# Moving the sums of the down-projection weights in a Strassen-Winograd feed-forward on one Trainium2 core

## The chip, the core and the metric

One core of a Trainium2 chip runs the whole program. The metric is device microseconds of one execution, start to end. The engines work side by side and each takes its instructions in the order written for it: TensorE (PE: matmuls; PEld: its weight loads), VectorE (DVE), ScalarE (ACT), GpSimd (POOL) and SyncE (SP), which issues all the transfers of this kernel. Engines wait for one another by semaphores. SBUF is the on-chip memory of 128 partitions, PSUM holds the matmul results in eight banks, DRAM is the memory outside.

## The reference

Two encoder layers of width 1024 run over 1024 prompt rows and 8 x 16 sample rows (1152 rows, nine tiles of 128). Each layer is attention, then a channel mixer; every sub-layer is modulated by a condition (adaLN) and closed by a scaled residual and a layer norm. The change lies in the channel mixer:

```python
u = h @ w_up                                  # 1024 -> 2 x 2816
y = conv_b + sum(conv_w[tap] * ue[:, tap:tap + T] for tap in range(3))
a, g = jnp.split(y, 2, axis=-1)
out = (jax.nn.gelu(g) * a) @ w_down           # 2816 -> 1024
x = layer_norm(DEEPNORM_ALPHA * x + (1 + g_f) * out, ln_g, ln_b)
```

`ue` is `u` with two earlier rows ahead of it. All is float32.

## The kernel before

**Precision.** Each matmul operand is split into a high part (a cast, by ScalarE, line 177) and a low remainder (a subtraction, mostly by VectorE, line 188), and each product is three matmuls: low x high, high x low, high x high. `wh`, `wl` are the two parts of weights, `xa`, `H` and `x2r` hold those of activations.

**The up stage** (`ffn`). The 2816 columns of each half of w_up are 22 blocks of 128; block j of the first half and block j of the gate half form pair j. Pairs 0 and 1 are computed plainly. Then `tsums` forms sums of the transposed activations, and pairs 2 to 21 run as a Strassen-Winograd scheme with seven half-sized products (`products`). A pair starts with two loads of 512 KB (lines 1369 and 1370, into a ring of four buffers, so two pairs), GpSimd forms four sums of weights (lines 1177 to 1180), and for each product the weight is split into one of six slots, TensorE does 2 x 12 matmuls (line 1229), and ScalarE or VectorE takes the two results out of PSUM, adding what is there (lines 1188, 1190, 1197). When a half of the pair is complete, `conv_row` applies the convolution (ScalarE line 1316, VectorE line 1277 for two taps, GpSimd line 1286 for sample rows), and `gated` does the GELU (ScalarE, line 1323) and the gating (GpSimd, line 1324) and stores the row block.

**Preparation for the down stage, done in the up stage.** The down-projection is Winograd's scheme too. `act_sums` forms, for two finished blocks, four sums of activations on GpSimd (lines 1336 to 1339) and stores them to `actS`. `weight_sums(m)` does it for blocks 2m and 2m+1 of w_down, with lo and hi halves of 512 columns: b11, b12 are the halves of block 2m, b21, b22 those of block 2m+1. It loads both blocks into the two buffers `w0` (tile w0f, line 1347), forms four sums in place on GpSimd (lines 1348 to 1351), and stores both buffers to the DRAM tensor `wT` (line 1353). It is called inside pair `wsum[m]` behind its third product; `wsum` is 2, 3, 4, 6, 8, ... 20. There is one pair of `w0` buffers, so set m+1 loads when set m is stored.

**The down stage** (`down`). Seven products run one after another, numbered 1, 2, 5, 6, 3, 7, 4, each over the eleven m, with four banks of prompt rows and, in products 1, 2, 5 and 6, a fifth for the sample rows. `fetch(q, m)` loads an activation operand and a weight half, splits them, and returns them. A weight half goes either into a buffer of the rings `early` and `late`, or, for stored sums, straight into the slot that its low part will take; there are six slots in products 1 to 6. Product 5 takes `wT[m, 0]`'s lo half for prompt rows and the hi half of block 2m for sample rows. Behind the products follow the residual and norm of each tile of 128 rows (`head`, `tail`); `homes` says into which buffer each tile's residual row block is loaded (line 1081). In layer 1 `tail` (lines 1530 to 1534 and 1004 to 1019) writes the output.

**Order.** The program is written in the order above, and a planner then orders each engine's instructions with a simulated timeline: an instruction whose inputs and buffers are ready may be placed ahead of others written before it. `issue_after(ins)` adds an edge that keeps those instructions of a block that run on the engine of `ins` behind `ins`. In layer 0 the adaLN weights of later stages are loaded and multiplied between the products (lines 226 and 234), and 16 copies of a bias table run (line 1657).

Of the kernel before, what the change touches and what calls it, by code (L numbers as in the profile page):

```python
# [102 lines left out]
class Trunk:  # L103
# [1140 lines left out]
    def ffn(self, l, xsrc, xdst, affs):  # L1244
        nc, I, O, H, F = self.nc, self.I, self.O, self.H, self.F
# [67 lines left out]
        def conv_row(u, j, gg, y):  # L1313
            cc = j + 22 * gg
            tap = tapper(cc)
            nc.scalar.activation(y, u[:, 2:1154], AF.Identity, bias=cw[:, cc, 3:4], scale=cw[:, cc, 2:3])  # L1316
            tap(y[:, 0:1024], u[:, 1:1025], 1)
            tap(y[:, 0:1024], u[:, 0:1024], 0)
            samples(y[:, 1024:1152], u[:, 1026:1154], cc, tap)
            rows(j, gg, u[:, 1024:1168])  # L1320

        def gated(j, ya, yg):
            nc.scalar.activation(yg, yg, AF.Gelu_apprx_tanh)
            nc.gpsimd.tensor_mul(yg, yg, ya)  # L1324
            if j % 2:
                nc.sync.dma_start(self.actD[j], yg)
                self.pend.append(j // 2)
            else:
                for r in (slice(0, 512), slice(1024, 1152)):
                    nc.sync.dma_start(self.actD[j][:, r], yg[:, r])  # L1330

        def act_sums():
            for m in self.pend:
                a11, a21 = ygate[0][:, 0:512], ygate[0][:, 512:1024]
                a12, a22 = ygate[1][:, 0:512], ygate[1][:, 512:1024]
                nc.gpsimd.tensor_add(a22, a21, a22)
                nc.gpsimd.tensor_sub(a21, a11, a21)
                nc.gpsimd.tensor_sub(a11, a22, a11)
                nc.gpsimd.tensor_sub(a12, a12, a11)
                for i in range(2):  # L1340
                    nc.sync.dma_start(self.actS[m, i], ygate[i][:, 0:1024])
            self.pend = []

        def weight_sums(m):
            b11, b12, b21, b22 = (t[:, o : o + 512] for t in self.w0 for o in (0, 512))
            for i in range(2):
                nc.sync.dma_start(self.w0[i], I["wdn"][l, 2 * m + i])
            nc.gpsimd.tensor_sub(b11, b12, b11)
            nc.gpsimd.tensor_sub(b12, b22, b12)
            nc.gpsimd.tensor_sub(b22, b22, b11)  # L1350
            nc.gpsimd.tensor_sub(b21, b22, b21)
            for i in range(2):
                nc.sync.dma_start(self.wT[l][m, i], self.w0[i])

        def plain(j):
            y = [yact, ygate[j % 2]]
# [10 lines left out]
        def spair(j):  # L1367
            sa, sg = self.ws.next(), self.ws.next()
            nc.sync.dma_start(sa, I["wup"][l, j])
            nc.sync.dma_start(sg, I["wup"][l, j + 22])  # L1370
            ua, ug = us.next(), us.next()
            y = []

            def after(i, q):
                if i % 2 == 0:
                    self.step(1)
                if i == 1:
                    act_sums()
                if i == 2 and j in wsum:
                    weight_sums(wsum.index(j))  # L1380
                if q == 4:
                    y.append(ygate[j % 2])
                    conv_row(ug, j, 1, y[0])

            self.products(sa, sg, ua, ug, (S1, S2, S3), p1s, sub, TT, after, "first" if j == NPL else None)
            ya = yact
            conv_row(ua, j, 0, ya)
            gated(j, ya, y[0])

        self.pend = []  # L1390
        wsum = [2, 3] + list(range(4, NFF - 1, 2))
# [9 lines left out]
        for j in range(NPL, NFF):  # L1401
            spair(j)
            if l == 0 and j == 2:
                self.tables_b(self.ws.next())
            if l == 0 and 3 <= j < 19:
                with self.tc.issue_after(self.pairmm):
                    self.skew_b(j - 3)
# [4 lines left out]
    def down(self, l, xsrc, xdst, affs, act_sums):  # L1412
        nc, I, F, H = self.nc, self.I, self.F, self.H
# [13 lines left out]
        narrow = self.ws  # L1427
        fa, fb = F[:, 4096:5120], F[:, 8320:9344]
        homes = {8: fa, 0: fb, 1: self.w0[1], 2: fa, 3: fb, 4: X2[:, 0:1024], 5: X2[:, 2048:3072], 6: fa, 7: fb}
        xs = {}  # L1430

        def rows(*ts):
# [3 lines left out]
        raws = [w[:, i * 512 : i * 512 + 512] for w in [self.w0[1]] + narrow.items for i in range(2)]  # L1436
        early = Ring(raws + [F[:, o : o + 512] for o in (0, 512, 1024)])
        late = Ring(raws)
        subs = self.subslots(ws[1:4])
        X1 = self.X1  # L1440
        acts = Ring([(X1[:, o : o + 640], X1[:, o + 640 : o + 1280]) for o in range(0, 8960, 1280)])
# [2 lines left out]
        wdn, wT, actD, actS = I["wdn"][l], self.wT[l], self.actD, self.actS  # L1444
        lo_half, hi_half = slice(0, 512), slice(512, 1024)

        def weight(src, ring=None):
            hi, lo = subs.next()
            raw = ring.next() if ring else lo.bitcast(F32)
            nc.sync.dma_start(raw, src)  # L1450
            self.split(raw, hi, lo, "a", "v")
            return hi, lo

        def act(src, sample=None):
            n = 512 if sample is None else 640
            hi, lo = (t[:, 0:n] for t in acts.next())
            raw = lo.bitcast(F32)
            nc.sync.dma_start(raw[:, 0:512], src)
            if sample is not None:
                nc.sync.dma_start(raw[:, 512:640], sample)  # L1460
            self.split(raw, hi, lo, "a", "v")
            return hi, lo
# [12 lines left out]
        def prompt(j, n):  # L1475
            return actD[j][:, n]

        def sample(j):
            return actD[j][:, 1024:1152]

        def fetch(q, m):
            e, o = 2 * m, 2 * m + 1
            w2 = None
            if q == 1:
                a, w = act(prompt(e, lo_half), sample(e)), weight(wdn[e][:, lo_half], early)
            elif q == 2:
                a, w = act(prompt(o, lo_half), sample(o)), weight(wdn[o][:, lo_half], early)
            elif q == 5:
                a, w = act(actS[m, 1][:, hi_half], sample(e)), weight(wT[m, 0][:, lo_half])
                w2 = weight(wdn[e][:, hi_half], late)  # L1490
            elif q == 6:
                a, w = act(actS[m, 0][:, lo_half], sample(o)), weight(wT[m, 1][:, hi_half])
                w2 = weight(wdn[o][:, hi_half], late)
            elif q == 3:
                a, w = act(actS[m, 1][:, lo_half]), weight(wdn[o][:, hi_half], late)
            elif q == 7:
                a, w = act(actS[m, 0][:, hi_half]), weight(wT[m, 0][:, hi_half])
            else:
                a, w = act(prompt(o, hi_half)), weight(wT[m, 1][:, lo_half])
            return a, w, w2 or w  # L1500

        def product(q, banks, bs=None, new=True, keep=0, hook=None):
            for m in range(NK - keep):
                a, w, w2 = fetch(q, m)
                for i in range(4):
                    mm(self.bank(banks[i]), a, i, w, new and m == 0, m == NK - 1)
                if bs is not None:
                    mm(self.bank(bs), a, 4, w2, q in (1, 5) and m == 0, q in (2, 6) and m == NK - 1)
                if hook:
                    hook(m)  # L1510
# [85 lines left out]
        subs = Ring(subs.items + more)  # L1596
# [15 lines left out]
        subs = Ring(subs.items[0 : NK - len(more)] + more if l == 0 else subs.items)  # L1612
        product(4, E, keep=keep, hook=tails(2))
        kept = [(m, fetch(4, m)) for m in range(NK - keep, NK)]
        for i in range(4):
            for m, (a, w, _) in kept:
# [303 lines left out]
```

## Time and profile before

| what | us |
|---|---|
| median of 3 runs | 2839.86 (2837.35 to 2843.75) |
| the profiled execution | 2844.65 |
| its span, first to last instruction | 2842.6 |
| TensorE busy | 2676.1 (94%) |
| VectorE busy | 2027.0 (71%) |
| ScalarE busy | 1348.0 (47%) |
| GpSimd busy | 1106.9 (39%) |
| DMA queue, share of 16 engines | 56.8% |

The up stage's pair loops run from 537.6 to about 1062 us (layer 0) and from 2075.3 to about 2566 us (layer 1), the down stages behind them to about 1345 and to the end. Rows of the profile name an engine, a line of the kernel, the operation, and what it writes and reads; the number behind an x is a count. In rows of stretches stand first the stretch and its length, then the busy time of each engine, then the clock granted to TensorE, the DMA engines' share and their rate. In square brackets stands how long the engine was idle before an instruction and what ended that. A row "A <- B: t, n, m" of the waits says that A waited for B t us in n waits, the longest m.

### The profile page before, as it was taken

How to read it: one execution, taken by the hardware profiler on the slowest of the kernel's cores; microseconds unless marked ns; L12 is line 12 of the kernel's file. 1: busy time of each engine (PE TensorE's matmuls, PEld its weight loads, DVE VectorE, ACT ScalarE, POOL GpSimd, SP SyncE). 2: the span in 40 equal slices, each digit the busy share in tenths (PEclk: the TensorE clock that was granted, in tenths of full speed). 3: DMA queues.
4: the chain of work that ended last, by engine and by line, in shares of the span. 5: the costliest groups of instructions: out<-in, count | busy, mean ns of one | idle time of the engine just before them, and what ended most of it. 6: DMA issues, size and time to landing. Idle time of an engine off the chain costs nothing. (4 is left out here: it accounts for less than half of the span.)

```text
span 2842.6 us, 47206 instructions
## 1 busy us (share of the span) xinstructions
PE 2676.1 (94%) x17134; PEld 2356.5 (83%) x17134; DVE 2027.0 (71%) x3850; ACT 1348.0 (47%) x2752; POOL 1106.9 (39%) x808
## 2 busy tenths in 40 slices
PE   7999889889999999999899999999988999999997
PEld 5897768878999997777798888767988999997775
DVE  4376767777776684588663677668888888885578
ACT  3475724433333344455636666652443344444454
POOL 2132523678554641013421111232489855551001
PEclk9999999999999999999999999999999999999998
DMA  8656434698554447675767457854565422237664
GB/s 291 213 159 197 141 129 156 209 329 283 183 175 156 163 133 236 225 248 196 267 201 257 122 156 198 225 162 146 178 206 196 177 81 96 85 116 239 216 218 156
DMA packets 252714, 534.35 MB, mean 188 GB/s; under 512 B 40032, under 2 KB 100400, under 8 KB 252480
## 3 DMA queue, kind: packets, MB, share of 16 engines
q1 hardware_dynamic: 252480, 531.32, 56.8%
q8 instruction: 135, 2.21, 0.3%
q14 instruction: 99, 0.81, 0.1%
HBM read 391.12 MB, written 149.54 MB: 190 GB/s over the span
## 5 line engine op out<-in xcount | busy, mean ns | idle before, releaser
L1229 PE MATMUL PS<-H,wh 128*128 128x256 f32 (+1 forms) x2624 | 409.7, 299 | 0.0
L1466 PE MATMUL PS<-wh,xa 128*128 128x512 f32 x1144 | 366.9, 399 | 11.9 <-DVE F L1584 5.3
L1229 PEld LDWEIGHTS PS<-H,wh 128*128 128x128 f32 x2624 | 374.4, 193 | 0.0
L1277 DVE SCALAR_TENSOR_TENSOR F<-F 128x1024 f32<-128x1024 f32 x320 | 312.9, 1025 | 28.1 <-ACT F L1316 27.8
L177 ACT CAST wh<-F 128x512 fp32r<-128x512 f32 (+2 forms) x234 | 137.1, 594 | 316.5 <-PE PS L1229 203.7
L1190 DVE TENSOR_TENSOR F<-PS,F 128x320 f32<-128x320 f32 (+1 forms) x446 | 196.6, 451 | 123.5 <-PE PS L1229 121.6
L188 DVE TENSOR_TENSOR wl<-F,wh 128x512 fp32r<-128x512 f32 (+2 forms) x234 | 238.6, 1029 | 56.0 <-ACT wh L177 54.3
L1466 PEld LDWEIGHTS PS<-wh,xa 128*128 128x128 f32 x1144 | 215.4, 189 | 69.5 <-ACT H L177 6.1
L1229 PE MATMUL PS<-H,wl 128*128 128x256 f32 (+1 forms) x1312 | 235.4, 301 | 24.4 <-ACT F L1197 15.3
L1466 PE MATMUL PS<-wl,xa 128*128 128x512 f32 x572 | 227.0, 397 | 0.2
L1229 PEld LDWEIGHTS PS<-H,wl 128*128 128x128 f32 x1312 | 196.6, 193 | 34.3 <-ACT F L1197 16.3
L1229 PE MATMUL PS<-xa,wh 128*128 128x320 f32 (+1 forms) x1328 | 207.5, 299 | 0.0
L188 DVE TENSOR_TENSOR xa<-xa 128x640 fp32r<-128x640 f32 (+1 forms) x154 | 122.5, 801 | 112.8 <-ACT xa L177 112.3
L1229 PEld LDWEIGHTS PS<-xa,wh 128*128 128x128 f32 x1328 | 189.8, 192 | 0.0
L1065 POOL TENSOR_TENSOR F<-F 128x1024 f32<-128x1024 f32 x24 | 62.7, 2611 | 308.2 <-ACT xa L177 148.9
L177 ACT CAST xa<-xa 128x640 fp32r<-128x640 f32 (+1 forms) x154 | 104.0, 682 | 162.8 <-DMA xa<-actD 110.8
L188 DVE TENSOR_TENSOR wl<-ws,wh 128x512 fp32r<-128x512 f32 (+1 forms) x149 | 166.2, 1120 | 10.3 <-ACT wh L177 10.2
L1316 ACT ACTIVATE F<-F 128x1152 f32<-128x1152 f32 x80 | 108.0, 1351 | 114.7 <-DVE F L1190 65.7
L177 ACT CAST wh<-ws 128x512 fp32r<-128x512 f32 (+1 forms) x167 | 113.1, 685 | 102.9 <-PE PS L1229 47.1
L640 POOL TENSOR_TENSOR F<-F,x2r 64x512 f32<-64x512 f32 x62 | 79.4, 1280 | 167.9 <-DVE F L616 145.6
L1324 POOL TENSOR_TENSOR F<-F 128x1152 f32<-128x1152 f32 x44 | 123.7, 2810 | 52.1 <-DVE F L1277 40.8
L1229 PE MATMUL PS<-xa,wl 128*128 128x320 f32 (+1 forms) x664 | 122.9, 307 | 21.2 <-DVE F L1190 20.7
(346 smaller groups left out, 6287.3 us busy)
## 6 DMA issues: line engine op xcount, KB each, us to landing
ws<-in_adaw_dram SPq DMA_DIRECT2D x64, 512.0 KB
ws<-in_wup_dram SPq DMA_DIRECT2D x49, 512.0 KB
F<-in_adaw_dram SPq DMA_DIRECT2D x48, 512.0 KB
w0f<-in_wdn_dram SPq DMA_DIRECT2D x44, 512.0 KB
wT<-w0f SPq DMA_DIRECT2D x44, 512.0 KB
actS<-F SPq DMA_DIRECT2D x44, 512.0 KB
xa<-actS SPq DMA_DIRECT2D x88, 256.0 KB
F<-in_wup_dram SPq DMA_DIRECT2D x39, 512.0 KB
```

The lines of the kernel that those rows point to most:

```text
L177: nc.scalar.copy(out, in_)
L188: self.eng(el).tensor_sub(lo, src, hi.bitcast(F32))
L640: self.eng("v" if last else "p").tensor_mul(on[r, q], on[r, q], rb[r, :])
L1065: self.eng(er[0]).tensor_mul(xr, x, self.lng)
L1190: nc.vector.tensor_add(d, v(ps), a if len(a.shape) == 3 else v(a))
L1229: self.pairmm = nc.tensor.matmul(ps[:, 0:m], w[a][:, k * 128 : k * 128 + 128], x(p, k, n), start=start and c == 0, stop=c == 11, skip_grou ...
L1277: nc.vector.scalar_tensor_tensor(o, u, cw[:, cc, i : i + 1], o, op0=ALU.mult, op1=ALU.add)
L1316: nc.scalar.activation(y, u[:, 2:1154], AF.Identity, bias=cw[:, cc, 3:4], scale=cw[:, cc, 2:3])
L1324: nc.gpsimd.tensor_mul(yg, yg, ya)
L1466: self.downmm = nc.tensor.matmul(ps, a[p][:, i * 128 : i * 128 + 128], w[q], start=first and c == 0, stop=last and c == 2, skip_group_chec ...
```

## The change

In `weight_sums` the instruction that formed the difference b12 - b11 is gone. b12 becomes b22 - b12, b22 becomes that plus b11, which is what b22 - (b12 - b11) was, and b21 becomes b22 - b21: three sums. Of block 2m's buffer only the hi half is stored. The call stands under an `issue_after` on the second load of its own pair, so that the set's loads and stores come behind that load on SP's queue; GpSimd's instructions get no such edge. In the down stage, product 5 loads both halves of block 2m of w_down into a ring of eight buffers, GpSimd forms the difference, and both are split as before. In layer 1 the residual row blocks 6 and 7 get buffers of their own in place of those of blocks 2 and 3.

```diff
             for i in range(2):
                 nc.sync.dma_start(self.w0[i], I["wdn"][l, 2 * m + i])
-            nc.gpsimd.tensor_sub(b11, b12, b11)
             nc.gpsimd.tensor_sub(b12, b22, b12)
-            nc.gpsimd.tensor_sub(b22, b22, b11)
+            nc.gpsimd.tensor_add(b22, b12, b11)
             nc.gpsimd.tensor_sub(b21, b22, b21)
-            for i in range(2):
-                nc.sync.dma_start(self.wT[l][m, i], self.w0[i])
+            nc.sync.dma_start(self.wT[l][m, 0][:, 512:1024], b12)
+            nc.sync.dma_start(self.wT[l][m, 1], self.w0[1])
...
-            nc.sync.dma_start(sg, I["wup"][l, j + 22])
+            pairdma = nc.sync.dma_start(sg, I["wup"][l, j + 22]).ins
...
                 if i == 2 and j in wsum:
-                    weight_sums(wsum.index(j))
+                    with self.tc.issue_after(pairdma):
+                        weight_sums(wsum.index(j))
...
         homes = {8: fa, 0: fb, 1: self.w0[1], 2: fa, 3: fb, 4: X2[:, 0:1024], 5: X2[:, 2048:3072], 6: fa, 7: fb}
+        if l:
+            homes[6], homes[7] = self.hf, self.gateS
...
         late = Ring(raws)
+        diffs = Ring([F[:, o : o + 512] for o in range(2048, 6144, 512)])
...
             elif q == 5:
-                a, w = act(actS[m, 1][:, hi_half], sample(e)), weight(wT[m, 0][:, lo_half])
-                w2 = weight(wdn[e][:, hi_half], late)
+                a = act(actS[m, 1][:, hi_half], sample(e))
+                r, b = diffs.next(), diffs.next()
+                nc.sync.dma_start(r, wdn[e][:, lo_half])
+                nc.sync.dma_start(b, wdn[e][:, hi_half])
+                nc.gpsimd.tensor_sub(r, b, r)
+                w, w2 = (subs.next() for _ in range(2))
+                self.split(r, *w, "a", "v")
+                self.split(b, *w2, "a", "v")
```

## The prediction

> **What bounds the kernel now.** I read the page first, then busy time by stretches, then the waits inside the stretches that lose time, then rows at single places. From the page, part 1 and part 2 (40 slices of 71 us):
>
> ```profile
> PE 2676.1 (94%) x17134; PEld 2356.5 (83%) x17134; DVE 2027.0 (71%) x3850; ACT 1348.0 (47%) x2752; POOL 1106.9 (39%) x808
> ...
> PE   7999889889999999999899999999988999999997
> ...
> POOL 2132523678554641013421111232489855551001
> ```
>
> TensorE is the bound, and what can be won is where its digit falls below 9. Two such places, slices 7 and 8 and slices 29 and 30, open the pair loops of the two feed-forward stages, and there POOL stands at 6 to 9 tenths. The GpSimd instructions that write w0f, which are the weight sums, and nothing else (columns: us, busy us and count, clock, DMA share, GB/s), first by four stretches, then by stretches cut at pair starts:
>
> ```profile
> 740.00:1060.00 320.00, 0.00 (x0) 1.00 0.46 155
> ...
> 2250.00:2560.00 310.00, 0.00 (x0) 1.00 0.28 98
> ```
>
> ```profile
> 537.60:574.60 37.00, 15.37 (x9) 0.86 0.72 252
> 574.60:609.80 35.20, 4.08 (x3) 0.93 1.02 368
> 609.80:743.50 133.70, 46.92 (x28) 0.98 0.77 264
> 2075.30:2112.20 36.90, 15.39 (x8) 0.81 0.70 238
> 2112.20:2250.50 138.30, 56.69 (x32) 0.94 0.54 192
> ```
>
> So the weight sums, written for pairs 2, 3, 4, 6, ... 20 of a layer, do not run there: all eleven sets of four instructions of a layer run ahead and are over when pair 8 begins. The same stretches with all engines, layer 1 and then layer 0:
>
> ```profile
> core 0: us, PE busy (x) PEld busy (x) DVE busy (x) ACT busy (x) POOL busy (x), PEclk, DMA share, GB/s
> 2075.30:2112.20 36.90, 27.47 (x168) 27.05 (x169) 29.35 (x49) 14.85 (x29) 31.93 (x26) 0.81 0.70 238
> 2112.20:2250.50 138.30, 121.26 (x843) 118.95 (x842) 125.18 (x126) 46.71 (x80) 125.21 (x79) 0.94 0.54 192
> ...
> 2272.80:2519.30 246.50, 246.50 (x1850) 246.38 (x1849) 211.99 (x276) 103.59 (x177) 142.88 (x100) 1.00 0.26 91
> ```
>
> ```profile
> 537.60:574.60 37.00, 28.20 (x203) 25.86 (x201) 26.36 (x46) 13.21 (x26) 24.67 (x22) 0.86 0.72 252
> 574.60:609.80 35.20, 25.76 (x204) 23.31 (x200) 24.60 (x34) 12.66 (x20) 20.49 (x15) 0.93 1.02 368
> 609.80:743.50 133.70, 129.96 (x997) 118.86 (x997) 99.87 (x120) 44.00 (x77) 113.87 (x79) 0.98 0.77 264
> 743.50:971.50 228.00, 227.97 (x1797) 209.38 (x1793) 165.39 (x237) 88.82 (x149) 118.70 (x86) 1.00 0.49 165
> ```
>
> A pair is 7 products x 2 column groups x 12 = 168 matmuls, so the stretches hold, in layer 1, one pair, five and eleven. In layer 0 the matmuls of the adaLN weights run between; counting line 1229 alone:
>
> ```profile
> 609.80:743.50 133.70, 119.99 (x841) 115.38 (x841) 0.98 0.77 264
> 743.50:971.50 228.00, 210.54 (x1513) 203.28 (x1513) 1.00 0.49 165
> ```
>
> That is five pairs and nine. A steady pair of layer 1 takes 246.5/11 = 22.4 us. The five pairs beside the sums take 138.3 - 5 x 22.4 = 26.2 us more than steady ones, the first pair 36.9 - 22.4 = 14.5 more. In layer 0 a steady pair is 228/9 = 25.3; the five pairs lose 133.7 - 126.7 = 7.0, the pair ahead of them 9.9, the first 11.7. Who ends TensorE's waits in the five pairs of layer 1, and what GpSimd's and ScalarE's work waits for in the steady ones:
>
> ```profile
> PE PS L1229 <- DVE F L1190: 17.0, 9, 5.6
> ```
>
> ```profile
> ACT wh L177 <- PE PS L1229: 82.9, 33, 2.9
> ...
> POOL F L1179 <- DVE wl L188: 23.4, 6, 3.9
> ```
>
> TensorE waits for VectorE's evictions, never for the weights. In steady pairs ScalarE's weight casts wait for TensorE to give slots back, so the splits are ahead. And why VectorE is late, from its groups in the five pairs and in the eleven:
>
> ```profile
> L1277 DVE SCALAR_TENSOR_TENSOR F<-F 128x1024 f32<-128x1024 f32 x21 | 38.4, 1830 | 0.9 <-ACT F L1316 0.8
> ...
> L1190 DVE TENSOR_TENSOR F<-PS,F 128x320 f32<-128x320 f32 x25 | 12.0, 481 | 1.2 <-PE PS L1229 1.2
> ```
>
> ```profile
> L1277 DVE SCALAR_TENSOR_TENSOR F<-F 128x1024 f32<-128x1024 f32 x45 | 66.1, 1469 | 10.7 <-ACT F L1316 10.7
> ...
> L1190 DVE TENSOR_TENSOR F<-PS,F 128x320 f32<-128x320 f32 x55 | 26.6, 483 | 4.7 <-PE PS L1229 4.7
> ```
>
> The convolution taps, with both inputs in SBUF, take 1830 ns beside the sums and 1469 without; the evictions, with one input in PSUM, take 481 and 483. GpSimd's sums slow VectorE's SBUF work, and evictions queue behind it. VectorE's busy time grew from 211.99/11 = 19.3 us a pair to 125.18/5 = 25.0, more than the 22.4 that TensorE needs: 5.8 x 5 = 28.8 us over 32 sum instructions, 0.90 us each. The lost time is 26.2/32 = 0.82 us each.
>
> **The change, part by part.** *The order.* The two loads of a set, and its two stores, go behind the second load of their own pair on SP's queue. The pair's loads wait for buffers, so the sets can no longer run ahead: one in each of pairs 2, 3, 4, then one in two pairs. *Fewer sums.* Three GpSimd instructions instead of four, one 256 KB store less of 1 MB. A pair with a set then costs VectorE 3 x 0.90 = 2.7 us on top of 19.3, so 22.0 against 22.4: just covered, with 3.1 us of free time in the next pair, which has none. This cover is thin, and the whole forecast hangs on it. GpSimd has room: 142.88/11 = 13.0 us a pair and 3 x 56.69/32 = 5.3 added. In layer 0 VectorE's cover is wider, 165.39/9 = 18.4 of 25.3.
>
> Term 1, the five pairs of layer 1 (26.2): two sets stay in them at the opening (pairs 3 and 4), where VectorE has no free time; I leave 2 x 3 x 0.82 = 5 and win 21. Bounds: 26 if those hide too, 2 if all 30 instructions behind pair 2 still cost 0.82 (26.2 - 24.6).
>
> Term 2, the first pair of layer 1 (14.5): 8 instructions of 0.82 lie in it, and 3 to 6 stay. I take 3; 0 to 8 is the bound, since the transposed sums of activations that open the stage stay.
>
> Term 3, layer 0. The five pairs lose 7.0 over 28 instructions, 0.25 each; six of them stay (1.5), so 5.5 are won. The 9.9 us of the pair before are a late pair load:
>
> ```profile
> 600.26 0.33 SPq L1369 DMA_DIRECT2D ws<-in_wup_dram  x1
> ```
>
> ```profile
> 607.97 1.14 ACT L177 CAST wh<-ws 128x512 fp32r<-128x512 f32 x2 [3.29 <-DMA ws<-in_wup_dram]
> ```
>
> ```profile
> 609.82 1.44 PE L1229 MATMUL PS<-H,wl 128*128 128x320 f32 x4 [5.66 <-DVE wl L188]
> ```
>
> The DMA engines are full there (share 1.02). The sums' transfers are part of that load, the bias table's copies are another and stay; I take 4 of the 9.9 (0 to 9.9). First pair 1 (0 to 4). Layer 0 together 10.5.
>
> Term 4, the fifth product of the down stage. The moved subtraction: one GpSimd instruction for each of 11 steps, ahead of the casts; its shortest form took this (min, median, max ns):
>
> ```profile
> L1348 POOL TENSOR_TENSOR w0f<-w0f x22: 1274/1742/2937, 521.1 to 2232.2; 128x512 f32<-128x512 f32 x22
> ```
>
> ```profile
> 2647.00:2686.00 39.00, 39.00 (x169) 31.38 (x168) 24.15 (x37) 20.51 (x35) 0.00 (x0) 1.00 0.71 231
> ```
>
> In layer 1 that product runs in about this stretch: GpSimd idle, VectorE 24.15 of 39 us. Should VectorE lose 1.27 us for each, 24.15 + 14.0 = 38.2 still fits in 39. Bytes loaded are the same (a half of w_down instead of a stored difference), and a ring of eight halves lets loads run four steps ahead. I take 0; the bounds are 0 and a loss of 11 x 0.82 = 9 a layer. The other side of w0's later release: the first weights of product 1 load into it, now behind pair 20's set instead of long before. A pair's time covers them; uncovered, 0 to 5.7 us a layer by the stall above.
>
> Term 5, the end of layer 1. Rows 6 and 7 of the residual get buffers of their own instead of those of rows 2 and 3, whose results must first be stored:
>
> ```profile
> 2813.78 0.32 SPq L1081 DMA_DIRECT2D F<-xd  x1
> ```
>
> ```profile
> 2817.32 1.06 ACT L1530 ACTIVATE F<-F 128x1024 f32<-128x1024 f32 x1 [11.47 <-DMA F<-xd]
> ```
>
> ```profile
> 2819.55 0.15 DVE L1009 TENSOR_SCALAR C<-C 128x1 f32<-128x1 f32 x1 [1.85 <-ACT F L1008]
> ```
>
> ScalarE stood 11.47 us behind that load, and VectorE, which works almost without a break to the end, lost 1.85 for it. I take 1.5 (0 to 4): VectorE's own chain is late next.
>
> The sum is 21 + 3 + 10.5 + 0 + 1.5 = 36 us. The profiled execution took 2844.65 us (its span 2842.6), so 2808.7; the median of the runs, 2839.86, is 4.8 below it, and for the median I forecast 2804.
>
> One rule speaks against it. The Trainium skill, SBUF — State Buffer, section Who interferes with whom, calls the port pair that VectorE and GpSimd share an exclusive lock, held for a whole instruction, which a VectorE instruction with two SBUF inputs needs against a GpSimd read. By it a pair with a set could pay 3 x 1.27 = 3.8 us, 23.1 against 22.4, and nine such pairs 6 us, which would make it 2810. The trace agrees in kind (1830 against 1469 ns with two inputs, 481 against 483 with one); its 0.90 us decides the size.
>
> **The rivals.** *Every sum costs wherever it stands.* If evictions are late behind any slowed tap, not only when VectorE is full, the price stays 0.82 and 0.25 us an instruction, and only eleven instructions a layer are saved: 9 + 3 + 1.5 = 13.5, so 2826. For it: VectorE is left 0.4 us of cover in pairs with a set, and the sums of activations fall in the same even pairs. Against it: steady pairs already have GpSimd at 13.0 of 22.4 us and lose nothing.
>
> *Slower: SP's queue.* A set's stores wait on SP for GpSimd, and SP issues in order; in the stretch 2057 to 2250 of layer 1:
>
> ```profile
> SPq L1353 <- POOL w0f L1349: 28.9, 11, 8.3
> ...
> SPq L1353 <- POOL w0f L1351: 15.5, 8, 3.1
> ```
>
> Today this ends with pair 8; then it would go on to pair 20, with the next pair's loads behind the stores. One late pair load cost 5.66 us above. The eight later sets of each layer decide from 36/16 = 2.3 us each; at 5.66 they cost 91 and give 2839.9 + 91 - 36 = 2895. Against it: 4.0 us of wait a set (44.4/11) is less than the slack of splits that wait for slots.
>
> *It does not do what it says:* the pair loads themselves run far enough ahead that the sets still bunch; only term 5 is left, 2838. Their buffers hold two pairs, which speaks against it.
>
> *More:* the openings of both layers clear up as well (terms 1 to 3 at their upper bounds, 26 + 8 + 16.9 + 4, and 1.5): 2783.
>
> **How the numbers follow.** The forecast 0.55 (its own range 2790 to 2818), every sum costs 0.20, more 0.09, no effect 0.04, slower 0.12. About 0.2%, 5.7 us, is what a measurement of this kernel can tell from no change. Faster is 0.55 + 0.20 + 0.09 = 0.84. The range runs from the case "more" to past the second, 2782 to 2834, and leaves out "no effect", "slower" and little of the rest.
>
> **What would show it.** Right: GpSimd's w0f work spread over the whole pair loop, pair time flat near 22.4 us from pair 5 of layer 1, VectorE near 22 us in even pairs; product 5 without TensorE idle; no ScalarE wait for F<-xd near the end. Wrong: even pairs over 23 us throughout, SP waits for GpSimd ahead of pair loads, or casts waiting for in_wup in late pairs.

## The result, and the profile after

| | median us (range) | profiled execution us | its span us |
|---|---|---|---|
| before, 16 runs | 2841.18 (2830.5 to 2847.31) | 2844.65 | 2842.6 |
| after, 16 runs | 2829.45 (2822.34 to 2838.91) | 2829.26 | 2827.4 |

The ratio of the times is 0.9961, 95% interval 0.9948 to 0.9974: the kernel became 0.39% or 11.7 us faster. The forecast was 36 us. The two profiled executions lie 15.2 us apart in span, more than the medians, because the profiled one of before lies 3.5 us above its median. Cut at the first and the last matmul of line 1229 in each pair loop, these 15.2 us stand here (minus is a gain):

| part | before | after | difference |
|---|---|---|---|
| pair loop of layer 0 | 527.0 | 516.3 | -10.7 |
| its end to the next matmul of line 1229 | 323.9 | 327.2 | +3.3 |
| those matmuls, between the two loops | 106.6 | 105.2 | -1.4 |
| their end to layer 1's pair loop | 580.2 | 578.7 | -1.5 |
| layer 1, pair 2 | 36.9 | 35.1 | -1.8 |
| layer 1, pairs 3 to 7 | 138.3 | 118.9 | -19.4 |
| layer 1, pairs 8 to 21 | 314.4 | 331.5 | +17.1 |
| layer 1's loop end to the end | 277.7 | 278.0 | +0.3 |

The rest, 1.1, lies ahead of layer 0's loop. Most of what was won in five pairs of layer 1 was lost again in the fourteen behind them. The page of the changed kernel, the busy times and GpSimd's line of slices:

```profile
PE 2664.8 (94%) x17134; PEld 2343.6 (83%) x17134; DVE 2024.4 (72%) x3850; ACT 1348.0 (48%) x2752; POOL 1105.9 (39%) x808
...
POOL 2121523466656642113511111232476667652101
```

GpSimd's hump behind slice 28 is now flat and twice as long. GpSimd has 808 instructions as before; one sum of four has only moved to the down stage. GpSimd's instructions on w0f in layer 1, by stretches cut at pair starts (pair 2, pairs 3 to 7, pairs 8 to 19), and then all engines in pair 2, in pairs 3 to 7 and in pairs 8 to 21:

```profile
2063.90:2099.00 35.10, 10.56 (x7) 0.85 0.58 210
2099.00:2217.90 118.90, 8.08 (x6) 1.00 0.34 122
2217.90:2504.80 286.90, 25.97 (x18) 0.99 0.36 127
```

```profile
2063.90:2099.00 35.10, 24.80 (x170) 24.39 (x169) 29.73 (x46) 15.10 (x29) 27.24 (x24) 0.85 0.58 210
2099.00:2217.90 118.90, 113.77 (x842) 111.86 (x841) 102.69 (x128) 46.93 (x80) 80.91 (x54) 1.00 0.34 122
2217.90:2549.40 331.50, 318.28 (x2354) 314.96 (x2353) 275.56 (x353) 134.30 (x229) 209.60 (x138) 0.99 0.37 130
```

Before, the last fourteen pairs were this row:

```profile
2250.50:2564.90 314.40, 313.78 (x2354) 313.39 (x2353) 268.62 (x353) 133.82 (x229) 175.10 (x120) 1.00 0.29 101
```

The sets are spread as the change says: 6 instructions in the five pairs instead of 32, 18 behind them instead of none. They stand in the pairs 4, 6, 8 and so on to 18; the pairs' loads run ahead of their pairs, and the sets go with them, so the last set, written for pair 20, runs in pair 18. But TensorE now stands idle 13.2 us in the last fourteen pairs, where it stood idle 0.6. The loss is not spread: the pairs 5 to 20 last in turn 25.7, 22.4, 25.1, 22.4, 27.0, 22.4, 25.1 us and so on. Two neighbours, pairs 10 and 11, after the change and then a like couple before it:

```profile
2267.30:2289.70 22.40, 22.40 (x170) 22.40 (x170) 19.91 (x25) 8.14 (x15) 16.07 (x11) 1.00 0.44 160
2289.70:2314.80 25.10, 23.11 (x170) 22.44 (x169) 20.97 (x26) 10.63 (x17) 16.07 (x12) 1.00 0.29 101
```

```profile
2250.50:2272.90 22.40, 22.40 (x171) 22.40 (x170) 19.09 (x25) 8.57 (x16) 15.03 (x11) 1.00 0.38 139
2272.90:2295.30 22.40, 22.40 (x170) 22.39 (x170) 19.46 (x26) 10.10 (x17) 11.29 (x9) 1.00 0.20 69
```

The slow pair is the odd one, behind the even pair in which the set's sums run, and VectorE is busy for 20.97 of its 25.10 us: no other engine is full. The column to read is GpSimd's before the change: 15.03 in the even pair, 11.29 in the odd one. The even pair also holds the four activation sums, and the change put the weight sums beside them. One such place, pairs 8 and 9 (pair 9 starts at 2240.3), on GpSimd, then on ScalarE, then on TensorE:

```profile
2234.07 1.29 POOL L1348 TENSOR_TENSOR w0f<-w0f 128x512 f32<-128x512 f32 x1 [4.24 <-DMA w0f<-in_wdn_dram]
2235.45 1.62 POOL L1349 TENSOR_TENSOR w0f<-w0f 128x512 f32<-128x512 f32 x1
2237.03 1.29 POOL L1336 TENSOR_TENSOR F<-F 128x512 f32<-128x512 f32 x1
2238.28 1.74 POOL L1350 TENSOR_TENSOR w0f<-w0f 128x512 f32<-128x512 f32 x1
2239.99 1.29 POOL L1337 TENSOR_TENSOR F<-F 128x512 f32<-128x512 f32 x1
2241.24 1.79 POOL L1179 TENSOR_TENSOR F<-ws 128x512 f32<-128x512 f32 x1
2242.99 2.27 POOL L1338 TENSOR_TENSOR F<-F 128x512 f32<-128x512 f32 x1
2245.22 1.33 POOL L1177 TENSOR_TENSOR F<-ws 128x512 f32<-128x512 f32 x1
2246.51 1.26 POOL L1339 TENSOR_TENSOR F<-F 128x512 f32<-128x512 f32 x1
```

```profile
2247.99 1.35 ACT L1316 ACTIVATE F<-F 128x1152 f32<-128x1152 f32 x1 [5.49 <-DMA actS<-F]
2249.25 0.68 ACT L1197 COPY F<-PS 128x320 f32<-128x320 f32 x2
```

```profile
2249.70 0.85 PE L1229 MATMUL PS<-H,wl 128*128 128x320 f32 x4 [2.86 <-ACT F L1197]
```

The three set sums (1348 to 1350) stand ahead of and between the activation sums (1336 to 1339), which work in place in the two `ygate` buffers and are then stored. The gate convolution of the even pair, ScalarE's line 1316, writes one of those buffers and so waits 5.49 us for the store. The evictions (line 1197) stand behind it in ScalarE's queue, and TensorE waits 2.86 us for a bank. No other is longer; over the pairs 5 to 19 TensorE waits 10.0 us for ScalarE's evictions of line 1197 and 7.7 for VectorE's. Whether the latter are late by the same chain is not shown:

```profile
PE PS L1229 <- ACT F L1197: 10.0, 7, 2.9
PE PS L1229 <- DVE F L1190: 7.7, 13, 1.5
```

### The profile page after: what moved, and what is told of

The parts are those of the page before. It is cut to its first block, busy times and chain, and to the rows that moved or that the text cites. A ratio compares the mean times of both kernels' runs of the same rounds, so it can differ in the third digit from the quotient of the medians.

```text
span 2827.4 us, 47181 instructions
## 1 busy us (share of the span) xinstructions
PE 2664.8 (94%) x17134; PEld 2343.6 (83%) x17134; DVE 2024.4 (72%) x3850; ACT 1348.0 (48%) x2752; POOL 1105.9 (39%) x808
## 5 line engine op out<-in xcount | busy, mean ns | idle before, releaser
L188 DVE TENSOR_TENSOR wl<-F,wh 128x512 fp32r<-128x512 f32 (+2 forms) x278 | 285.5, 1037 | 79.9 <-ACT wh L177 71.4
L1277 DVE SCALAR_TENSOR_TENSOR F<-F 128x1024 f32<-128x1024 f32 (+1 forms) x320 | 298.4, 977 | 32.1 <-ACT F L1316 31.6
L177 ACT CAST wh<-F 128x512 fp32r<-128x512 f32 (+2 forms) x278 | 163.3, 598 | 328.9 <-PE PS L1229 179.6
L188 DVE TENSOR_TENSOR xa<-xa 128x640 fp32r<-128x640 f32 (+1 forms) x154 | 129.5, 847 | 110.8 <-ACT xa L177 109.9
L1316 ACT ACTIVATE F<-F 128x1152 f32<-128x1152 f32 x80 | 108.0, 1350 | 104.5 <-DVE F L1190 39.6
L1324 POOL TENSOR_TENSOR F<-F 128x1152 f32<-128x1152 f32 x44 | 122.7, 2788 | 72.1 <-ACT F L1323 29.1
L177 ACT CAST wh<-ws 128x512 fp32r<-128x512 f32 (+1 forms) x153 | 104.6, 693 | 94.6 <-PE PS L1229 46.3
L188 DVE TENSOR_TENSOR wl<-ws,wh 128x512 fp32r<-128x512 f32 (+1 forms) x135 | 141.2, 1052 | 5.6 <-ACT wh L177 5.4
L319 PE MATMUL PS<-xa,H 128*128 128x512 f32 x504 | 134.1, 407 | 6.2 <-ACT xa L177 3.3
```

What stands on the lines that cost most here:

```text
L177: nc.scalar.copy(out, in_)
L188: self.eng(el).tensor_sub(lo, src, hi.bitcast(F32))
L319: self.nc.tensor.matmul(out[:, 0:n], H[:, p, j * kn + k, t0 : t0 + 128], w[a][:, k * n : k * n + n], start=i == 0, stop=i == 23,)
L1277: nc.vector.scalar_tensor_tensor(o, u, cw[:, cc, i : i + 1], o, op0=ALU.mult, op1=ALU.add)
```

## The experiments

Three theories stand in the expectations. A: the set's sums cost by meeting the activation sums in GpSimd's queue. B, the prediction's second case: each sum instruction costs its price wherever it stands. C, formed when the first runs had partly contradicted both: the victim is the chain activation sums, store, gate convolution, eviction, and whatever lengthens it in an even pair costs, by whichever queue. In the table, "loop" is the time from the first to the last matmul of a pair loop, in one profile. The kernel before was timed anew beside each group of kernels, so the ratios compare, not the medians. Kernels with the same code in a loop show how far one profile can be trusted: layer 0's loop differs by 2.5 us between `after` and `e9_mix` and by 4.6 between `e10_late` and `e12_homes`, layer 1's by 1.3 over the four with odd pairs and three sums.

| kernel | median us | ratio to before (95%) | loop, layer 0 | loop, layer 1 |
|---|---|---|---|---|
| before | 2841.18 to 2844.17 | 1 | 527.0 | 489.5 |
| after | 2829.45 | 0.9961 (0.9948 to 0.9974) | 516.3 | 485.5 |
| e1_odd | 2819.05 | 0.9921 (0.9901 to 0.9940) | 521.7 | 471.5 |
| e5_actfirst | 2837.75 | 0.9987 (0.9971 to 1.0002) | 519.7 | 490.1 |
| e4_orderonly | 2840.95 | 0.9992 (0.9977 to 1.0007) | 522.9 | 488.3 |
| e2_nosums | 2814.38, one run | | 515.7 | 476.3 |
| e9_mix | 2815.85 | 0.9898 (0.9882 to 0.9915) | 518.8 | 471.7 |
| e3_noorder | 2840.63 | 0.9987 (0.9972 to 1.0002) | 529.0 | 486.1 |
| e7_noact | 2790.36, one run | | 517.8 | 461.1 |
| e10_late | 2813.87 | 0.9886 (0.9868 to 0.9903) | 517.4 | 472.3 |
| e11_four | 2826.16 | 0.9938 (0.9922 to 0.9954) | 525.0 | 476.2 |
| e12_homes | 2813.36 | 0.9897 (0.9881 to 0.9913) | 512.8 | 472.8 |

Diffs are against the changed kernel where nothing else is said.

**The later sets in odd pairs.**

```diff
-        wsum = [2, 3] + list(range(4, NFF - 1, 2))
+        wsum = [2, 3] + list(range(5, NFF, 2))
```

> The changed kernel with the weight sets behind the loads of the odd pairs 5, 7, ... 21 instead of 4, 6, ... 20 (2 and 3 stay). Theory A: in layer 1 a set delays the activation sums that GpSimd forms in the same stretch, and through them the next gate convolution on ScalarE and an eviction behind it, 2.7 to 4.6 us for each of eight sets. Away from the activation sums a set costs nothing: every pair of layer 1 from the fourth on takes 22.4 to 22.8 us, and the kernel is 15 to 24 us faster than the changed one. Theory B: a set costs 0.8 us per instruction wherever it stands, because it slows VectorE: the pairs with a set, or those behind them, keep taking about 25 us, and the time stays within 4 us of the changed kernel. Layer 0 is the same under both.

Layer 1's loop fell from 485.5 to 471.5 us, its pairs from pair 3 on lasting 22.4 to 23.9. The instructions are the same in kind and number; only their place differs. ScalarE's waits of line 1316 for the last activation sum in pairs 5 to 19, after the change and then here:

```profile
ACT F L1316 <- POOL F L1339: 26.7, 7, 4.2
```

```profile
ACT F L1316 <- POOL F L1339: 5.4, 2, 2.8
```

B fell: the same sums cost 14.0 us less of that loop in the other pairs. A held for the loop and for the wait; TensorE's waits for evictions (lines 1197 and 1190) fell from 17.7 us to 3.4 as well. By the ratios the gain is about 11 us, less than the 15 to 24 that A gave, and pairs of up to 23.6 us are left where A had 22.8. Pairs 3 to 21 of layer 1, after the change and then with odd pairs:

```profile
2099.00:2549.40 450.40, 432.04 (x3194) 426.82 (x3193) 378.25 (x480) 181.23 (x309) 290.51 (x191) 1.00 0.36 128
```

```profile
2096.20:2532.70 436.50, 431.04 (x3194) 425.77 (x3193) 384.16 (x479) 180.38 (x309) 287.73 (x193) 1.00 0.38 135
```

VectorE is busy 5.9 us longer in the kernel whose stretch is 13.9 us shorter: how full it is does not set the time here. Layer 0 took 5.4 us more than after the change, little more than the 4.6 between equal ones; two of its pairs, 15 and 19, last 27.1 and 26.8.

**The sets held behind the activation sums on GpSimd** (pairs above 4).

```diff
-                nc.gpsimd.tensor_sub(a12, a12, a11)
+                self.lastsum = nc.gpsimd.tensor_sub(a12, a12, a11).ins
...
-                    with self.tc.issue_after(pairdma):
+                    with ExitStack() as es:
+                        es.enter_context(self.tc.issue_after(pairdma))
+                        if j > 4:
+                            es.enter_context(self.tc.issue_after(self.lastsum))
```

> The changed kernel with GpSimd's three instructions of a set (from pair 4 on) kept behind the last activation sum of the same pair on GpSimd's queue. Theory A: the wait of ScalarE's convolution (line 1316) for the last activation sum and for the store to actS falls from about 27 us in layer 1 to under 10, and layer 1's pair loop gets 12 to 24 us shorter. Theory B: the same number of instructions slows VectorE as before; pairs of 25 us stay and the time changes by less than 4 us.

This was a miss. The wait that A names fell to 4.5 us, and layer 1's loop stayed at 490.1, odd pairs at 25.2 to 26.9. Now VectorE's evictions are late. TensorE's waits in pairs 5 to 19, then GpSimd's row of a set's last sum with the pair's own sums behind it, VectorE's of the convolution taps beside these with the eviction behind them, and the same taps with odd pairs, with GpSimd's rows beside and behind them, where the set comes 11 us after the taps begin:

```profile
PE PS L1229 <- DVE F L1190: 17.1, 7, 2.7
```

```profile
2298.82 1.74 POOL L1350 TENSOR_TENSOR w0f<-w0f 128x512 f32<-128x512 f32 x1
2301.69 1.36 POOL L1178 TENSOR_TENSOR F<-F,ws 128x512 f32<-128x512 f32 x1
2303.13 2.13 POOL L1180 TENSOR_TENSOR ws<-ws,F 128x512 f32<-128x512 f32 x1
```

```profile
2299.32 6.07 DVE L1277 SCALAR_TENSOR_TENSOR F<-F 128x1024 f32<-128x1024 f32 x4
2305.92 0.48 DVE L1190 TENSOR_TENSOR F<-PS,F 128x320 f32<-128x320 f32 x1
```

```profile
2378.01 4.01 DVE L1277 SCALAR_TENSOR_TENSOR F<-F 128x1024 f32<-128x1024 f32 x4
```

```profile
2382.17 0.54 POOL L1286 TENSOR_TENSOR F<-F 128x16 f32<-128x16 f32 x1 [2.92 <-DVE F L1277]
...
2389.35 1.59 POOL L1348 TENSOR_TENSOR w0f<-w0f 128x512 f32<-128x512 f32 x1 [2.05 <-DMA w0f<-in_wdn_dram]
```

The same taps take 6.07 us beside GpSimd's sums and 4.01 where GpSimd stands idle for 2.92 of them. The set, put between the activation sums and the next pair's own weight sums (lines 1177 to 1180), runs into the taps, and pushes those sums into them too. So A was incomplete: moving the set out of the activation sums' way helps only if it does not land on the taps. With odd pairs it runs from 15.8 us into the pair on, beside no activation sum and after the taps of the pair's first half.

**The order alone,** on the kernel before (four sums, stored difference, old buffers):

```diff
-            nc.sync.dma_start(sg, I["wup"][l, j + 22])
+            pairdma = nc.sync.dma_start(sg, I["wup"][l, j + 22]).ins
...
-                    weight_sums(wsum.index(j))
+                    with self.tc.issue_after(pairdma):
+                        weight_sums(wsum.index(j))
```

> The kernel before with one part of the change alone: the sets' transfers behind their pair's second load. Four sums a set, product 5 and the row buffers as before. Theory A: four instructions in place of three beside the activation sums, so the slow pairs of layer 1 take 26 to 28 us instead of 25 to 27, 1 to 1.5 us more for each of eight sets, 8 to 12 us more in that loop; the down stages are what they were before the change (323.9 us from the last pair of layer 0 to the first shared key/value pair, against 327.2 with the change). Together 5 to 10 us slower than the changed kernel. Theory B: 0.8 us more a set and 0.25 in layer 0, 9 us more in the loops.

The odd ones of the pairs 5 to 17 of layer 1 last 25.6 to 26.3 us, the even ones behind pair 4 22.4, and the ratio's interval holds no change: what the opening wins is given back. Those seven odd pairs take 180.1 us together with four sums in a set, and 179.2 after the change with three, so their number has little to do with it. A had expected 8 to 12 us more in layer 1's loop than after the change; 2.8 more were measured.

**The sets without their sums.** The three sums of each set are left out, its loads and stores stay.

```diff
-            nc.gpsimd.tensor_sub(b12, b22, b12)
-            nc.gpsimd.tensor_add(b22, b12, b11)
-            nc.gpsimd.tensor_sub(b21, b22, b21)
```

> The changed kernel without GpSimd's three instructions of a set: the loads and the stores to wT stay, so the stored tensor holds the plain weights and the output is not the reference's. If the loss of layer 1 comes from SP's queue or the transfers, its slow pairs stay at 25 to 27 us. If it comes from GpSimd's instructions (theories A and B alike), all pairs from the fourth on take 22.4 us and layer 1's loop is 24 us shorter than with the change, 461 instead of 485.5; layer 0's loop changes by less than 4.

The slow odd pairs stayed, at 23.8 to 26.2 us (pairs 5 to 19): neither A nor B had that, and of the cases in the expectation the one that names SP's queue or the transfers held. One such place, on SP, GpSimd, ScalarE and TensorE in this order:

```profile
2311.46 0.33 SPq L1348 DMA_DIRECT2D wT<-w0f  x1
2311.89 0.38 SPq L1326 DMA_DIRECT2D actD<-F  x1
```

```profile
2306.27 2.68 POOL L1324 TENSOR_TENSOR F<-F 128x1152 f32<-128x1152 f32 x1 [1.53 <-DVE F L1277]
2315.07 1.29 POOL L1336 TENSOR_TENSOR F<-F 128x512 f32<-128x512 f32 x1 [6.13 <-DMA actD<-F]
```

```profile
2322.18 1.35 ACT L1316 ACTIVATE F<-F 128x1152 f32<-128x1152 f32 x1 [5.03 <-DMA actS<-F]
```

```profile
2331.49 0.86 PE L1229 MATMUL PS<-xa,wl 128*128 128x320 f32 x4 [2.28 <-DVE F L1190]
```

The set's store, which waits for the set's own load here, stands on SP right ahead of the store of the activations. These are ready at 2308.95 (line 1324), but their store is issued at 2311.89. The activation sums wait for it, since they overwrite that buffer. The same chain is late by another queue, and GpSimd is idle meanwhile; the eviction that is late at its end is one of VectorE's, behind the taps that follow the late convolution. From this came C.

**The chain without activation sums.** The four sums of lines 1336 to 1339 are left out; the stores stay.

```diff
-                nc.gpsimd.tensor_add(a22, a21, a22)
-                nc.gpsimd.tensor_sub(a21, a11, a21)
-                nc.gpsimd.tensor_sub(a11, a22, a11)
-                nc.gpsimd.tensor_sub(a12, a12, a11)
```

> The changed kernel, sets in the even pairs, without GpSimd's four activation sums (their stores stay and store the plain activations, so the output is not the reference's). Theory C: with nothing for a set to meet, every pair of layer 1 from the fourth on takes 22.4 to 22.8 us, and the loop is 18 to 25 us shorter than 485.5. Theory B: the pairs with a set still pay 2.5 us, and the loop stays over 480.

Pairs 3 to 21 of layer 1:

```profile
2085.40:2511.50 426.10, 425.48 (x3192) 424.75 (x3191) 370.75 (x481) 182.04 (x309) 228.26 (x152) 1.00 0.38 134
```

TensorE is idle 0.6 us there, and the sets stand in even pairs as after the change. Each pair from the fourth on lasts 22.3 to 22.8 us. VectorE's busy time is only 7.5 us lower than after the change while the stretch is 24.3 us shorter. C held, and layer 1's loop is 24.4 us shorter than after the change: the weight sums in even pairs cost by meeting the activation sums. The run does not tell the two ways apart in which they do: without activation sums neither is the gate convolution late nor are sums pushed into the taps, and GpSimd has less to do altogether. And C as worded does not cover the run with the sets held back, where it is not the convolution but VectorE's taps that are late.

**The change without the order.**

```diff
-                    with self.tc.issue_after(pairdma):
-                        weight_sums(wsum.index(j))
+                    weight_sums(wsum.index(j))
```

> The change without its order: three instructions a set, product 5 and the row buffers as changed, but the sets are free to run ahead as before. The sets bunch in the first seven pairs of each layer again. By 0.82 us for each instruction in layer 1 and 0.25 in layer 0, eleven instructions less a layer are worth 9 and 3 us: layer 1's loop 480, layer 0's 524, and the time 12 us under the kernel before.

The ratio's interval holds no change, where a fixed price would have given 12 us for the eleven fewer sums a layer. In pairs 3 to 7 of layer 1, the first window below, 24 sums instead of 32 make 136.6 us of 138.3:

```profile
2104.20:2240.80 136.60, 119.55 (x843) 117.66 (x843) 119.87 (x126) 46.71 (x81) 109.53 (x72) 0.95 0.54 188
```

VectorE's busy time fell from 125.18 to 119.87, the time of the stretch by 1.7. Layer 0's first pair became longer, 41.3 us; why is open. So neither the order alone nor the sum moved alone gains what can be measured; the whole change gains 0.39%.

**Odd pairs in layer 1 only, and the sets of layer 0 begun later.** The first edit, and then the second one, each against the changed kernel:

```diff
-        wsum = [2, 3] + list(range(4, NFF - 1, 2))
+        wsum = [2, 3] + list(range(4 + l, NFF - 1 + l, 2))
```

> Sets behind the even pairs in layer 0, as the change has them, and behind the odd pairs in layer 1. Theory C: layer 1 pays where a set meets the activation sums in one pair (the even ones), whatever the way; layer 0 has 3 us a pair of other matmuls that hide it, and there the odd pairs make it a little worse. So layer 0's pair loop takes 516 us as with the change (odd pairs: 521.7) and layer 1's 471 as with odd pairs in both (485.5 with the change): 5 us faster than odd pairs in both, about 2814, and 15 faster than the change. Theory B, a fixed price for each instruction wherever it stands, has been refuted for layer 1 if this holds.

```diff
-        wsum = [2, 3] + list(range(4, NFF - 1, 2))
+        wsum = [2, 3] + list(range(5, NFF, 2)) if l else list(range(6, 13)) + list(range(14, NFF, 2))
```

> As the mixed version, and in layer 0 the first sets stand behind pairs 6, 7, 8, ... 12, 14, ... 20 instead of 2, 3, 4, 6, ... 20, so that none runs in the opening. If the sets lengthen the opening of layer 0 (first pair 34.4 us with them, 31.0 without any), the first two pairs get 2 to 4 us shorter and the whole 2 to 4 faster than the mixed version. If the opening belongs to the transposed sums and the bias table's copies, no change within 1 us.

The first gives 518.8 and 471.7 us in the loops, within 3 us of what was expected. The second takes layer 0's first two pairs from 34.3 and 30.7 to 31.6 and 27.1, but pairs 4 and 11 last 29.5 and 29.1 there (28.1 and 25.4 after the change); its loop, at 517.4, is no shorter than after the change (516.3). At 0.9886 and 0.9898 the two are not told apart, so the 2 to 4 us expected of the later sets are neither shown nor ruled out. With `e12_homes` below, these are the fastest complete kernels, 1.0% to 1.1% under the time before.

**The moved sum undone,** with the sets placed as in the last kernel: four sums in the set, both blocks stored whole, product 5 from the stored difference.

```diff
+            nc.gpsimd.tensor_sub(b11, b12, b11)
             nc.gpsimd.tensor_sub(b12, b22, b12)
-            nc.gpsimd.tensor_add(b22, b12, b11)
+            nc.gpsimd.tensor_sub(b22, b22, b11)
...
-                r, b = diffs.next(), diffs.next()
...
+                a, w = act(actS[m, 1][:, hi_half], sample(e)), weight(wT[m, 0][:, lo_half])
```

> The version with late sets in layer 0 and odd pairs in layer 1, with the moved sum put back: four sums in the up stage, product 5 from the stored difference. Theory C: an odd pair of layer 1 had 11.3 us of GpSimd's work without a set (an even one 15.0); three instructions bring it to about 15.7, four to about 17.3, over what the even pairs carry, so pairs with a set take 0.5 to 1 us more and layer 1's loop 477 to 482 instead of 472. The down stages change by less than 2 us either way. Together 4 to 10 us slower than with three. If the moved sum costs in the down stage what it saves above, no difference.

The ratio is 0.9938 against 0.9886, the profiled spans lie 9.5 us apart (2823.1 and 2813.6), with 3.9 more in layer 1's loop (472.3 to 476.2) and 7.6 more in layer 0's (517.4 to 525.0, with pairs of 30.4 and 27.6). From layer 0's loop to the next matmul of line 1229 it takes 326.8 with the stored difference and 326.5 with the moved one: there, forming it in the down stage costs nothing that shows. From layer 1's loop to the end it is otherwise, first with the moved difference and then with the stored one:

```profile
2533.60:2813.60 280.00, 249.96 (x1059) 198.81 (x1057) 190.39 (x324) 133.04 (x220) 39.93 (x23) 0.97 0.62 203
2548.30:2823.10 274.80, 250.12 (x1059) 198.95 (x1057) 186.40 (x324) 134.01 (x220) 22.84 (x12) 0.96 0.63 208
```

That is 5.2 us, where less than 2 were expected either way. Over the kernels here the stage took 277.0 to 281.9 us with the moved difference and 274.8 to 278.8 with the stored one, so the move may cost a few us in layer 1. One profile of each does not prove it, and why is open.

**The old residual buffers,** placed as in the same kernel:

```diff
-        if l:
-            homes[6], homes[7] = self.hf, self.gateS
```

> The same version with rows 6 and 7 of the residual in layer 1 back in the buffers of rows 2 and 3. From the last matmul to the end it took 20.4 us in the profiles with and without the new buffers, so I expect no difference in the time (under 0.2%), and ScalarE's wait for the load of a row block back near 11 us. By the prediction's term 5 it would be 1.5 us slower.

ScalarE's wait near the end, after the change and then here, where it is back:

```profile
ACT F L1539 <- DMA F<-xd: 0.5, 1, 0.5
```

```profile
ACT F L1537 <- DMA F<-xd: 12.8, 2, 11.2
```

The time from the last matmul to the end is 20.4 us with and 20.3 us without the new buffers, and the ratios, 0.9897 and 0.9886, are not told apart. No price of the wait shows.

## Why the prediction was right and wrong

- *Term 1, the five pairs of layer 1:* 21 forecast, 19.4 measured, with six set instructions left in them, as said. That the size came out is in part luck. The 5 us left over were meant for VectorE's loss beside these sums in pairs 3 and 4, but the sums stand in pairs 4 and 6. Against 22.4, pairs 3 and 4 lose 0.9 us together, and 6.0 of the 6.9 lost stand in pairs 5 and 7, the slow odd ones of the next point.
- *The cover of the later sets in layer 1:* this is the step that failed, "just covered" in the forecast and a loss of 17.1 us in the trace. It was argued as VectorE's 22.0 us of work against TensorE's 22.4, and as GpSimd's 13.0 us of a pair plus 5.3. The sum of busy times did fit: VectorE was busy only 20.97 us in a slow pair of 25.10. What failed is taking that sum, an average over pairs, for the cover. The average of 13.0 hid two kinds of pairs, 15.03 and 11.29, and the even one holds a chain with a date: the store of the activations, four sums in place, a store, the convolution that overwrites the buffer, and evictions queued behind it. Steady pairs "lose nothing" at 13.0 said nothing about that chain. Moving the sets by one pair (layer 1's loop 485.5 to 471.5 us) and leaving out the activation sums (461.1) both took the loss away. The sign named for a miss, even pairs over 23 us, came in the odd ones, where TensorE meets the late eviction. The sentence in the second case that the activation sums fall in the same even pairs had the right place, but took it for a matter of VectorE's cover.
- *Term 2, the first pair of layer 1:* 3 forecast, 1.8 measured. Seven set instructions still run in it, against the 3 to 6 forecast. Without any sums it takes 30.7, but with four of them (odd pairs) still 35.0 and with eight (the order alone) 33.3, so the number of sums does not explain it. What does is open.
- *Term 3, layer 0:* 10.5 forecast, 10.7 measured (8.2 by the run `e9_mix`, with the same layer 0); by parts 2.7 in the first pair (1 forecast), 4.5 in the next (4), 4.3 in the five (5.5), and 0.8 lost behind them. The row of the second stretch:

```profile
570.80:601.50 30.70, 25.26 (x204) 23.21 (x200) 24.31 (x33) 11.36 (x18) 14.96 (x12) 0.96 1.03 378
```

The DMA engines are still full in it (1.03), eight copies of the bias table among the transfers.

- *Term 4, product 5:* nothing forecast, and nothing found in the product itself, though layer 1's whole stage may pay a few us (the run with the moved sum undone). TensorE works through the stretch in which product 5 runs, with GpSimd's five instructions in it; compare VectorE's 24.15 of before:

```profile
2631.50:2670.50 39.00, 39.00 (x169) 31.37 (x168) 24.49 (x37) 21.21 (x36) 7.13 (x5) 1.00 0.63 206
```

- *Term 5, the end:* 1.5 forecast, nothing measured. The wait went as said (11.5 us became 0.5), and the time from the last matmul to the end stayed at 20.4 us. The 1.85 us read as VectorE's loss was not won; that VectorE's chain, named as late next, is the whole bound fits this, but no run tests it.
- *Every sum costs wherever it stands:* its 2826 is the nearest forecast to 2829.45, by luck, since its mechanism is refuted: `e1_odd` has all the sums of the changed kernel, and its loop in layer 1 is 14.0 us shorter.
- *SP's queue:* SP still waits for the sets' sums, as in this row of layer 1's loop, but no cast of weights waits for a load in pairs 5 to 19:

```profile
SPq L1352 <- POOL w0f L1350: 36.5, 11, 4.2
```

The queue did matter in the kernel without sums, through another store.
- *The lock rule:* it priced a pair with a set at 23.1 us; 25.1 were measured in the pair behind, by the other mechanism, and without activation sums pairs with a set last 22.4. The row that prices a sum on VectorE is this: in pairs 3 to 21, VectorE is busy 378.25 us with 24 set instructions and 364.71 without them, 0.56 us each, below the 0.90 read from the crowded stretch:

```profile
2085.30:2530.90 445.60, 430.58 (x3194) 428.38 (x3193) 364.71 (x478) 178.75 (x309) 236.22 (x165) 0.99 0.36 127
```

By the rule in the Trainium skill, SBUF — State Buffer, section Who interferes with whom, up to a whole instruction of GpSimd (1.26 us for the shortest in the rows above) could be paid by VectorE. The trace agrees in kind, as the taps at 6.07 and 4.01 us show; the average price, 0.56 us a sum, stays under that bound.

The terms as forecast add to 36; as measured 19.4 + 1.8 + 10.7 - 17.1 + 0.4 for the rest make the 15.2 of the spans. Also open, beside layer 1's opening: the stage from layer 0's loop to the next matmul of line 1229, 3.3 us longer after the change, lasts 324 to 330 us over the kernels here, and no run told why.

## What to carry to other kernels

Work moved into "free" time has to be checked against the pair or iteration it lands in, not against an average: look whether neighbouring iterations differ (15.03 and 11.29 us on one engine here), and which chain in the fuller one has a buffer to free by a date. A buffer that is summed in place, stored and then overwritten ties several queues together, and a delay on any of them can reach the bound engine though no other engine is full. Where the work has the same amount anyway, try its phase first: here a shift by one pair took 14 us off layer 1's loop, and the whole change 4.0.

## What was not expected of the hardware

On average over a stretch, a GpSimd sum lengthened VectorE's busy time by a different amount according to where it stood: 0.90 us in the crowded opening, 0.56 over pairs 3 to 21, and 0.72 with odd pairs ((384.16 - 364.71) / 27). And VectorE's busy time did not order the kernels: over those pairs 378.25 us went with 450.4, 384.16 with 436.5, and 364.71, without the sums, with 445.6.
